# Gates of a mixer block in pairs by seven half-size products

## Chip, cores and metric

The kernel runs on 1 core of one Trainium2 chip. The metric is the time on the device in microseconds, the median of several executions.

## What is computed

One layer of a transformer-like block on 512 tokens of width 1024, in f32. The input is normalised (h) and multiplied by one wide matrix; the first columns feed four branches (attention, spatial gating, short convolution, pooling), the last 4096 columns are the pre-activations of four gates of width 1024. Then:

```python
gates = jax.nn.sigmoid(gate_pre + gate_b[l]).reshape(B_, S_, N_BRANCH, D_)
merged = (gates[:, :, 0] * y_a + gates[:, :, 1] * y_b
          + gates[:, :, 2] * y_c + gates[:, :, 3] * y_d)
x = x + rmsnorm(merged @ w_out[l], norm_mix_post[l])
h = rmsnorm(x, norm_ffn_pre[l])
f = jnp.square(jax.nn.relu(h @ w_ff1[l])) @ w_ff2[l]
x = x + rmsnorm(f, norm_ffn_post[l])
```

where y_a to y_d are the branches' outputs (256 wide) times a 256 x 1024 matrix each.

## The kernel before

Everything is kept transposed: features on the 128 partitions, the 512 tokens along the row. Each f32 operand is split into a high and a low piece of the type fp32r (`split_w`: ScalarE copies the high piece `wh`, VectorE subtracts for the low piece `wl`); `mm3` makes three TensorE products of every pair of operands, high by high, high by low, low by high. Weights come as tiles of 128 x 1024 f32 by SP's queue into a ring of three `raw` buffers and are split into five `wh`/`wl` buffers. `split_by_dma` (L122) spares VectorE the subtraction: ScalarE writes the negated high piece into `lo`, and a transfer that POOL issues adds the weight to it.

The scheduler of the framework orders each engine's instructions by priority (program order) as their inputs and buffers come free; TensorE alone keeps the order of the program (`InOrder`, L102), and ScalarE for a part of the head.

The stages, in order: the head, the branches and attention (to about 152 us); the gates; the output product with wO and the two norms; the feed-forward part; the end.

The gates (L679 to L682): for each of the 8 blocks b of 128 output features, four gate tiles (`gate`, L449; `feature_block`, L329: 8 K tiles x 3 products of 512 columns, tile `fb`, then a multiplication by the row `rbc` into a `g` tile), some of block 0 during attention. Then `merge(b)` (L457): four sigmoids, for each branch 6 products of 512 columns (tile `y`), multiplied by the gate and summed, the result split into `mh`, `ml`. L683 to L686 ask for gmix, gffn and x, which have room of their own, so that they come early.

The feed-forward part: the first `EARLY` = 4 tiles of w1 are multiplied by the first half of the tokens (`ff1`, L718, tile `z`) while the second half is still being normalised, then by the second half. The other 28 tiles go in pairs by a scheme of seven half-size products (Strassen's, in Winograd's form; L855 to L897): a pair is a 2 x 2 matrix of blocks (K halves by tile), the tokens' halves and K halves give the blocks A11, A12, A22 and the sums S1 to S4, made once. `part` (L849) is one step: 4 K tiles x 3 products of 256 columns into a bank `pa`, `pb`, `pc` or `pd`; VectorE makes four combinations of the weights in place in `raw`, and the results are put together from PSUM. Between the steps stand steps of the second product (`second`, L807, tile `acc`, 12 products of 512 columns).

Of the kernel before, what the change touches and what calls it, by code (L numbers as in the profile page):

```python
# [18 lines left out]
P = 128  # L19
S = 512  # L20
# [60 lines left out]
def build(ctx, tc, d, out):  # L81
# [40 lines left out]
    def split_by_dma(src):  # L122

        raw = load(src)
        hi = wp.tile([P, 1024], F32R, tag="wh", name="wh", bufs=5)
        lo = wp.tile([P, 1024], F32R, tag="wl", name="wl", bufs=5)
        ACT.copy(hi, raw)
        ACT.activation(lo, f(hi), AF.Copy, scale=-1.0)
        POOL.dma_start(lo, src.bitcast(F32R), accum_op=ALU.add)
        return hi, lo  # L130
# [187 lines left out]

    s3 = ExitStack()
# [349 lines left out]
    xp = ctx.enter_context(tc.tile_pool(name="xp", bufs=1, reuse_waits="tile", **right))  # L669
    x1 = xp.tile([P, NT, D], F32, name="x1")  # L670
    r2 = xp.tile([P, TOP], F32, name="r2")[:, :NT]
    mp = ctx.enter_context(ExitStack())
    mpool = mp.enter_context(tc.tile_pool(name="mp", bufs=1, reuse_waits="tile", **right))
    mh = mpool.tile([P, KD, S], F32R, name="mh")
    ml = mpool.tile([P, KD, S], F32R, name="ml")
    mT = (mh, ml)
    gmix = mpool.tile([P, D], F32, name="gmix")
    gffn = mpool.tile([P, D], F32, name="gffn")
# [17 lines left out]
    HK, HS = KD // 2, S // 2  # L696
# [9 lines left out]
    wk_ = ws.enter_context(tc.tile_pool(name="wk", bufs=1, reuse_waits="tile"))  # L706
# [316 lines left out]
```

## Time and profile before

| | us |
|---|---|
| median of 3 executions | 744.18 (743.61 to 745.3) |
| the profiled execution | 744.92 |
| its span in the profile | 743.2 |
| TensorE busy | 728.5 |
| VectorE busy | 467.2 |
| ScalarE busy | 356.5 |

The span is what the profile covers; the execution's own time is 1.7 us longer. Matmuls overlap in the engine, so the durations of single ones (389 ns for 512 columns) are longer than the time from one to the next. "Idle before" in a row is the time for which the engine did nothing before that instruction, and the name behind the arrow is what ended it. The windows view has the engines in the order TensorE (PE), its weight loads (PEld), VectorE (DVE), ScalarE (ACT), POOL, and behind them the granted TensorE clock as a share of full speed, the share of DMA time and GB/s.

### The profile page before, as it was taken

To read this page: it belongs to the slowest core of one execution; us is meant where nothing else is said; L and a number is where in the kernel's file an instruction comes from. 1 tells how busy PE (TensorE), PEld (TensorE's weight loads), DVE (VectorE), ACT (ScalarE), POOL (GpSimd) and SP (SyncE) were. 2 spreads that over 40 slices of the span, in tenths; PEclk is the share of its full clock that TensorE was granted. 3 is DMA by queue.
4 is the path that set the end of the run, shared out by engine and by line. 5 is a ranking of instruction groups with operands and counts; after the bars stand their busy time and mean duration, and the time that the engine had idled before them with its cause. 6 is when DMAs were issued, how large, how long until landed. Compare 5 with 4: busy or idle time off the path is not lost.

```text
span 743.2 us, 10315 instructions
## 1 busy us (share of the span) xinstructions
PE 728.5 (98%) x4058; PEld 636.4 (86%) x4058; DVE 467.2 (63%) x760; ACT 356.5 (48%) x584; POOL 15.9 (2%) x32
## 2 busy tenths in 40 slices
PE   8999999999999999999997999999999999999996
PEld 8998788888888888888887899999999999888885
DVE  7599986355456365365355976777677676774424
ACT  6875444523323232332346756546665556753411
POOL 1110000000000000000011000000000000000001
PEclk9999999999999999999999999999999999999999
DMA  8523222362232322323137033322433233533103
GB/s 304 183 107 114 86 95 73 117 219 94 90 109 86 112 86 90 109 86 111 44 101 198 1 108 120 101 99 86 130 97 114 86 101 127 170 113 112 60 0 114
DMA packets 23728, 80.87 MB, mean 109 GB/s; under 512 B 3072, under 2 KB 3584, under 8 KB 23680
## 3 DMA queue, kind: packets, MB, share of 16 engines
q1 hardware_dynamic: 23072, 78.12, 31.2%
q0 software_dynamic: 608, 2.10, 1.6%
q8 instruction: 32, 0.52, 0.3%
q14 instruction: 16, 0.13, 0.1%
HBM read 78.11 MB, written 2.10 MB: 108 GB/s over the span
## 4 chain that ended last, share of the span: by engine, by line
PE 88%; DVE 5%; DMA 2%; ACT 2%; issue 1%; SPq 0%; POOL 0%; DVEq 0%; ACTq 0%; POOLq 0%
PE fb L95 28%; PE acc L95 23%; PE pa L95 8%; PE y L95 6%; PE wo L95 5%; PE pc L95 5%; PE pd L95 3%; PE pb L95 2%; PE psA L95 2%; PE sgv L95 2%; DMA xT<-in_xT 1%; PE po L95 1%; DMA wl<-in_w 1%; DMA raw<-in_wF 1%; DVE wl L119 1%
## 5 line engine op out<-in xcount | busy, mean ns | idle before, releaser
L95 ACT CAST wh<-raw 128x1024 fp32r<-128x1024 f32 (+2 forms) x154 | 153.7, 1009 | 222.3 <-issue 105.4
L119 DVE TENSOR_TENSOR wl<-raw,wh 128x1024 fp32r<-128x1024 f32 (+2 forms) x150 | 173.8, 1167 | 28.8 <-ACT wh L95 26.5
L95 PE MATMUL fb<-zh,wh 128*128 128x512 f32 x336 | 131.4, 391 | 0.1
L95 PE MATMUL fb<-zl,wh 128*128 128x512 f32 x336 | 130.8, 389 | 0.0
L95 PE MATMUL fb<-zh,wl 128*128 128x512 f32 x336 | 130.8, 389 | 0.0
L95 PE MATMUL acc<-wh,ul 128*128 128x512 f32 x232 | 90.5, 390 | 1.2 <-DVE ul L798 1.2
L95 PE MATMUL acc<-wh,uh 128*128 128x512 f32 x232 | 90.7, 391 | 0.0
L95 PE MATMUL acc<-wl,uh 128*128 128x512 f32 x232 | 90.6, 391 | 0.0
L452 DVE TENSOR_TENSOR g<-fb,rbc 128x512 f32<-128x512 f32 x32 | 22.1, 692 | 96.7 <-PE fb L95 96.7
L798 DVE TENSOR_TENSOR ul<-u,uh 128x512 fp32r<-128x512 f32 x58 | 38.7, 689 | 57.2 <-ACT uh L95 57.1
L95 PEld LDWEIGHTS fb<-zh,wl 128*128 128x128 f32 x336 | 63.1, 188 | 13.2
L95 PEld LDWEIGHTS fb<-zh,wh 128*128 128x128 f32 x336 | 63.1, 188 | 13.2 <-DVE zc L361 0.4
L95 PEld LDWEIGHTS fb<-zl,wh 128*128 128x128 f32 x336 | 63.1, 188 | 12.8
L95 PEld LDWEIGHTS acc<-wh,ul 128*128 128x128 f32 x232 | 43.6, 188 | 11.4 <-DVE ul L798 2.1
L95 PEld LDWEIGHTS acc<-wh,uh 128*128 128x128 f32 x232 | 43.6, 188 | 8.5 <-ACT uh L95 0.4
L95 ACT CAST uh<-u 128x512 fp32r<-128x512 f32 x58 | 34.3, 618 | 34.2 <-PE acc L95 33.7
L95 PEld LDWEIGHTS acc<-wl,uh 128*128 128x128 f32 x232 | 43.6, 188 | 7.9
L95 ACT ACTIVATE u<-u 128x512 f32<-128x512 f32 x60 | 33.2, 622 | 16.3 <-DVE u L890 16.3
L95 PE MATMUL pa<-hsh,wh 128*128 128x256 f32 x112 | 31.3, 280 | 0.5 <-ACT x L95 0.5
L95 PE MATMUL pa<-hsl,wh 128*128 128x256 f32 x112 | 31.2, 279 | 0.0
L95 PE MATMUL pa<-hsh,wl 128*128 128x256 f32 x112 | 31.2, 279 | 0.0
L95 PE MATMUL wo<-wh,mh 128*128 128x512 f32 x64 | 25.1, 392 | 0.0
(313 smaller groups left out, 1419.7 us busy)
## 6 DMA issues: line engine op xcount, KB each, us to landing
raw<-in_w SPq DMA_DIRECT2D x64, 512.0 KB, 3.5
raw<-in_wG SPq DMA_DIRECT2D x32, 512.0 KB, 3.4
raw<-in_wF SPq DMA_DIRECT2D x10, 512.0 KB, 4.1
raw<-in_wB SPq DMA_DIRECT2D x8, 512.0 KB, 3.4
raw<-in_wO SPq DMA_DIRECT2D x8, 512.0 KB, 3.4
xk<-in_x SPq DMA_DIRECT2D x4, 512.0 KB, 9.3
x<-in_x SPq DMA_DIRECT2D x4, 512.0 KB, 5.8
wl<-in_w POOLq DMA_DIRECT2D x4, 512.0 KB, 6.5
```

The lines of the kernel that those rows point to most:

```text
L95: ins = op(*a, **k)
L119: DVE.tensor_tensor(lo[:, :n], raw[:, :n], f(hi)[:, :n], ALU.subtract)
L452: DVE.tensor_tensor(g, ps, rbc, ALU.mult)
L798: DVE.tensor_tensor(ul, u[j], f(uh), ALU.subtract)
```

## The change

Blocks 0 and 1 of the gates stay. For blocks 2 to 7 the seven-product scheme of the feed-forward part is made into a generator, `seven`, and the four gate tiles of a block go through it as two pairs. What that needs is added: `z_sums` makes the sums of z (`zsum`) during block 1, and the quarter of z that is used no more (first K half, second half of the tokens) is overwritten with the last form; the low piece of the right tile's second half (`w22`) is made by `split_by_dma`, also that of wB from block 1 on, in buffers of its own. `merge` becomes a generator as well: the products y of block b-1 are put between the steps of the first pair of block b. The merged result is kept in one tile for each block (`mT`) instead of one large tile, x, gmix and gffn get room that the gates used before, and are asked for when that is free. In the feed-forward part, `ff1` makes all products with the high piece of the weight first, tiles 2 and 3 of w1 are split by VectorE, the first tile of w2 is asked for before the first pair's weights, and the first three steps of the second product stand inside the first pair. The diff, cut:

```diff
--- before.py
+++ after.py
...
-    def split_by_dma(src):
-        raw = load(src)
-        hi = wp.tile([P, 1024], F32R, tag="wh", name="wh", bufs=5)
-        lo = wp.tile([P, 1024], F32R, tag="wl", name="wl", bufs=5)
-        ACT.copy(hi, raw)
-        ACT.activation(lo, f(hi), AF.Copy, scale=-1.0)
-        POOL.dma_start(lo, src.bitcast(F32R), accum_op=ALU.add)
+    def split_by_dma(src, raw=None, n=1024, own=None):
+        raw = load(src, n) if raw is None else raw
+        if own is None:
+            hi = wp.tile([P, 1024], F32R, tag="wh", name="wh", bufs=5)
+            lo = wp.tile([P, 1024], F32R, tag="wl", name="wl", bufs=5)
+        else:
+            hi, lo = [own.tile([P, 1024], F32R, tag=f"b{c}", name=f"b{c}", bufs=1) for c in "hl"]
+        ACT.copy(hi[:, :n], raw[:, :n])
+        ACT.activation(lo[:, :n], f(hi)[:, :n], AF.Copy, scale=-1.0)
+        POOL.dma_start(lo[:, :n], src.bitcast(F32R), accum_op=ALU.add)
...
+    HK, HS = KD // 2, S // 2
+    B1, B2 = slice(0, 512), slice(512, 1024)
+    def part(ps, w, at, a, first):
+        for k in range(HK):
+            mm3(ps[:, :HS], sl(w, slice(None), slice(at + k * P, at + (k + 1) * P)), sl(a, slice(None), k),
+                first and k == 0, k == HK - 1, not first)
+    def seven(srcs, forms, small, g, h, by_dma):
+        A11, A12, A22, S1, S2, S3, S4 = forms
+        left, rght = load(srcs[0]), load(srcs[1])
+        w = split_w(left)
+        w22 = split_by_dma(srcs[1][:, B2], rght[:, B2], 512) if by_dma else split_w(rght[:, B2], 512)
+        DVE.tensor_tensor(left[:, B1], rght[:, B1], left[:, B1], ALU.subtract)
+        DVE.tensor_tensor(rght[:, B1], rght[:, B2], rght[:, B1], ALU.subtract)
+        DVE.tensor_tensor(rght[:, B2], rght[:, B2], left[:, B1], ALU.subtract)
+        DVE.tensor_tensor(left[:, B2], left[:, B2], rght[:, B2], ALU.subtract)
+        wl = split_w(left)
+        wr = split_w(rght)
+        pa, pb = bank("pa"), bank("pb")
+        part(pa, w, 0, A11, True)
+        x1 = small()
+        ACT.copy(x1, pa[:, :HS])
+        yield
+        part(pb, w, 512, A12, True)
+        DVE.tensor_tensor(g[:, :HS], pb[:, :HS], x1, ALU.add)
+        yield
+        pc = bank("pc")
+        part(pc, wl, 0, S1, True)
+        x5 = small()
+        ACT.copy(x5, pc[:, :HS])
+        yield
+        part(pa, wr, 512, S2, False)
+        x2 = small()
+        ACT.copy(x2, pa[:, :HS])
+        yield
+        pd = bank("pd")
+        part(pd, wl, 512, A22, True)
+        yield
+        part(pc, w22, 0, S4, False)
+        DVE.tensor_tensor(h[:, :HS], pc[:, :HS], x2, ALU.add)
+        yield
+        part(pa, wr, 0, S3, False)
+        x3 = small()
+        ACT.copy(x3, pa[:, :HS])
+        DVE.tensor_tensor(g[:, HS:], pd[:, :HS], x3, ALU.add)
+        DVE.tensor_tensor(h[:, HS:], x3, x5, ALU.add)
+        yield
+    def forms(x, sums):
+        lo, hi, t0, t1 = slice(0, HK), slice(HK, KD), slice(0, HS), slice(HS, S)
+        return [sl(x, slice(None), k, t) for k, t in ((lo, t0), (hi, t0), (hi, t1))] + [
+            sl(sums, slice(None), c) for c in range(3)] + [sl(x, slice(None), lo, t1)]
...
-    def merge(b):
-        for i, g in enumerate(gates):
+    def merge(b, w):
+        gs = list(gates)
+        gates.clear()
+        for i, g in enumerate(gs):
             ACT.activation(g, g, AF.Sigmoid, bias=k1("gateb")[:, i * 8 + b:i * 8 + b + 1])
-        w = weights(d["wB"][b])
         prev = None
-        for i, br in ((1, bT), (2, cT), (3, dT), (0, aT)):
-            g = gates[i]
+        for i, br in ((1, bT), (2, cT), (3, dT), (0, aT)) if b == 0 else enumerate((aT, bT, cT, dT)):
+            g = gs[i]
             ps = bank("y")
             for k in range(2):
                 mm3(ps, sl(w, slice(None), slice((2 * i + k) * P, (2 * i + k + 1) * P)),
...
             if prev is not None:
                 DVE.tensor_tensor(g, g, prev, ALU.add)
             prev = g
-        ACT.copy(mh[:, b, :], prev)
-        DVE.tensor_tensor(ml[:, b, :], prev, f(mh)[:, b, :], ALU.subtract)
-        gates.clear()
+            yield
+        ACT.copy(mT[0][b], prev)
+        DVE.tensor_tensor(mT[1][b], prev, f(mT[0][b]), ALU.subtract)
...
+    zsum = [ss.tile([P, 3, HK, HS], F32R, name=f"zs{c}") for c in "hl"]
...
+    def z_sums(hh):
+        q = tqp.tile([P, 4, 2, HS], F32, name=f"q{hh}")
+        a11, a12, a21, a22 = (q[:, c] for c in range(4))
+        for c, (k, t) in enumerate(((0, 0), (HK, 0), (0, HS), (HK, HS))):
+            ix = slice(None), slice(k + 2 * hh, k + 2 * hh + 2), slice(t, t + HS)
+            DVE.tensor_tensor(q[:, c], f(zh)[ix], f(zl)[ix], ALU.add)
+        DVE.tensor_tensor(a22, a21, a22, ALU.add)
+        DVE.tensor_tensor(a21, a11, a21, ALU.subtract)
+        DVE.tensor_tensor(a11, a22, a11, ALU.subtract)
+        DVE.tensor_tensor(a12, a12, a11, ALU.subtract)
+        for c, v in enumerate((a22, a11, a21)):
+            ix = slice(None), c, slice(2 * hh, 2 * hh + 2)
+            ACT.copy(zsum[0][ix], v)
+            DVE.tensor_tensor(zsum[1][ix], v, f(zsum[0])[ix], ALU.subtract)
+        lower.append(a12)
+    steps = merge(0, weights(d["wB"][0]))
+    for i in range(4):
+        next(steps)
+    rest(steps)
+    for i in range(4):
+        gates.append(gate(1, i))
+        if i % 2 == 0:
+            z_sums(i // 2)
+    for hh, v in enumerate(lower):
+        ix = slice(None), slice(2 * hh, 2 * hh + 2), slice(HS, S)
+        ACT.copy(zh[ix], v)
+        DVE.tensor_tensor(zl[ix], v, f(zh)[ix], ALU.subtract)
+    tq.close()
+    merged("mp1", False)
+    ops = forms(z, zsum)
+    w = split_by_dma(d["wB"][1], own=wbp)
+    for b in range(2, KD):
+        steps = merge(b - 1, w)
+        for i in (0, 2):
+            g, h = (gp.tile([P, S], F32, tag="g", name="g", bufs=6) for _ in range(2))
+            for n, _ in enumerate(seven((d["wG"][4 * b + i], d["wG"][4 * b + i + 1]), ops, small_g, g, h, True)):
+                if i == 0 and n in (1, 2, 4, 5):
+                    next(steps)
+                if i == 0 and n == 5:
+                    rest(steps)
+                    w = split_by_dma(d["wB"][b], own=wbp)
+            for x in (g, h):
+                DVE.tensor_tensor(x, x, rbc, ALU.mult)
+            gates.extend((g, h))
+    rest(merge(KD - 1, w))
+    s4.close()
+    s1.close()
-    for b in range(KD):
-        while len(gates) < 4:
-            gates.append(gate(b, len(gates)))
-        merge(b)
-    nc.sync.dma_start(gmix, d["gmix"].partition_broadcast(P))
-    nc.sync.dma_start(gffn, d["gffn"].partition_broadcast(P))
-    for t in range(NT):
-        nc.sync.dma_start(x1[:, t, :], d["x"][t * P:(t + 1) * P, :])
-    s1.close()
...
+    gmix = wk_.tile([P, D], F32, name="gmix")
+    gffn = wk_.tile([P, D], F32, name="gffn")
+    nc.sync.dma_start(gmix, d["gmix"].partition_broadcast(P))
+    nc.sync.dma_start(gffn, d["gffn"].partition_broadcast(P))
+    for t in range(NT):
+        nc.sync.dma_start(x1[:, t, :], d["x"][t * P:(t + 1) * P, :])
...
     def ff1(j, w, ps, lo, hi):
-        for k in range(KD):
-            mm3(ps[:, lo:hi], sl(w, slice(None), slice(k * P, (k + 1) * P)), sl(h2, slice(None), k, slice(lo, hi)),
-                k == 0, k == KD - 1)
+        for c, parts in ((0, (0, 1)), (1, (0,))):
+            for k in range(KD):
+                for p in parts:
+                    PE.matmul(ps[:, lo:hi], w[c][:, k * P:(k + 1) * P], h2[p][:, k, lo:hi],
+                              start=c == 0 and k == 0 and p == 0, stop=c == 1 and k == KD - 1)
...
-        w, ps = split_by_dma(d["w1"][j]), bank("z")
+        w, ps = (split_by_dma if j < 2 else weights)(d["w1"][j]), bank("z")
...
-    w2 = {}
+    w2 = {0: weights(d["w2"][0, 0])}
     def second():
         j, us_ = pend.pop(0)
-        if j % 2 == 0:
+        if j and j % 2 == 0:
...
-        if j == EARLY - 1:
-            second()
...
+    ops = forms(h2, hsum)
     for j in range(EARLY, NFF, 2):
...
+        for n, _ in enumerate(seven((d["w1"][j], d["w1"][j + 1]), ops, small, g, h, False)):
+            if n == 4 or n in (1, 2) and j == EARLY:
+                second()
...
```

## Rows read from the trace of the kernel before

**Rows 1.** The page, part 1: busy time, share and instructions of each engine.
```profile
PE 728.5 (98%) x4058; PEld 636.4 (86%) x4058; DVE 467.2 (63%) x760; ACT 356.5 (48%) x584; POOL 15.9 (2%) x32
```

**Rows 2.** Windows: stretch, its length, each engine's busy time (instructions), clock, DMA.
```profile
157.32:179.08 21.76, 21.76 (x98) 18.02 (x97) 9.03 (x11) 6.67 (x9) 0.00 (x0) 1.00 0.43 154
184.52:347.72 163.20, 163.20 (x722) 135.13 (x721) 84.30 (x103) 50.34 (x61) 0.00 (x0) 1.00 0.29 97
392.90:406.50 13.60, 9.86 (x81) 9.45 (x80) 6.49 (x13) 8.08 (x14) 2.28 (x3) 1.00 0.94 219
406.50:425.80 19.30, 18.09 (x144) 17.24 (x143) 17.97 (x23) 13.77 (x23) 0.00 (x0) 1.00 0.03 13
460.05:475.35 15.30, 15.30 (x111) 14.31 (x110) 10.91 (x16) 9.04 (x16) 0.00 (x0) 1.00 0.33 101
```

**Rows 3.** The chain that ended last: start us, us, what, count.
```profile
157.32 21.76 PE fb L95 x96
179.08 5.44 PE y L95 x24
...
460.05 1.40 PE pa L95 x12
...
467.05 2.75 PE acc L95 x12
```

**Rows 4.** Timeline of VectorE, one feed-forward pair: start us, us, instruction, [idle before].
```profile
517.12 0.42 DVE L886 TENSOR_TENSOR u<-pc,x 128x256 f32<-128x256 f32 x1 [0.97 <-PE pc L95]
518.09 1.22 DVE L119 TENSOR_TENSOR wl<-raw,wh 128x1024 fp32r<-128x1024 f32 x1 [0.55 <-ACT wh L95]
519.49 1.22 DVE L119 TENSOR_TENSOR wl<-raw,wh 128x1024 fp32r<-128x1024 f32 x1 [0.18 <-ACT wh L95]
520.63 0.42 DVE L890 TENSOR_TENSOR u<-pd,x 128x256 f32<-128x256 f32 x1
520.97 0.41 DVE L891 TENSOR_TENSOR u<-x 128x256 f32<-128x256 f32 x1
523.83 1.29 DVE L798 TENSOR_TENSOR ul<-u,uh 128x512 fp32r<-128x512 f32 x2 [2.44 <-ACT uh L95]
...
525.57 2.36 DVE L119 TENSOR_TENSOR wl<-raw,wh 128x1024 fp32r<-128x1024 f32 x2
527.97 0.69 DVE L861 TENSOR_TENSOR raw<-raw 128x512 f32<-128x512 f32 x1
528.69 0.69 DVE L862 TENSOR_TENSOR raw<-raw 128x512 f32<-128x512 f32 x1
```

**Rows 5.** Timeline of VectorE, the merge of block 7.
```profile
344.37 1.36 DVE L468 TENSOR_TENSOR g<-g,y 128x512 f32<-128x512 f32 x2
...
349.12 1.22 DVE L119 TENSOR_TENSOR wl<-raw,wh 128x1024 fp32r<-128x1024 f32 x1
350.26 0.68 DVE L473 TENSOR_TENSOR ml<-g,mh 128x512 fp32r<-128x512 f32 x1
```

**Rows 6.** Timeline of ScalarE, a feed-forward pair.
```profile
475.20 2.20 ACT L95 ACTIVATE u<-u 128x512 f32<-128x512 f32 x4 [1.36 <-DVE u L890]
...
486.42 1.06 ACT L95 CAST wh<-raw 128x1024 fp32r<-128x1024 f32 x1 [3.52 <-PE pc L95]
```

**Rows 7.** The page, part 6: a gate weight's load, count, size, us to landing.
```profile
raw<-in_wG SPq DMA_DIRECT2D x32, 512.0 KB, 3.4
```

**Rows 8.** The tile `wl`: its four POOL transfers, from issue to landing.
```profile
DMA to landing us min/median/max: 5.6/6.5/7.6
```

**Rows 9.** Timeline of TensorE, the first products of the feed-forward part.
```profile
399.48 0.39 PE L95 MATMUL z<-hh,wl 128*128 128x256 f32 x1 [2.48 <-DMA wl<-in_w]
...
403.83 0.39 PE L95 MATMUL z<-hh,wl 128*128 128x256 f32 x1 [1.26 <-DMA wl<-in_w]
...
406.39 0.28 PE L95 MATMUL z<-hh,wl 128*128 128x256 f32 x1
```

**Rows 10.** Timeline of VectorE at the same place.
```profile
407.77 1.29 DVE L731 TENSOR_TENSOR hl<-tr,hh 128x512 fp32r<-128x512 f32 x2 [5.20 <-ACT hh L95]
```

More of the change, by code (lines that the diff above doesn't have):

```diff
@@ L668, in build @@
     TOP = 20
-    xp = ctx.enter_context(tc.tile_pool(name="xp", bufs=1, reuse_waits="tile", **right))
-    x1 = xp.tile([P, NT, D], F32, name="x1")
[L671 to L677, printed above, removed]
@@ L678, in build, with merged @@
-    gffn = mpool.tile([P, D], F32, name="gffn")
-    for b in range(KD):
-        while len(gates) < 4:
-            gates.append(gate(b, len(gates)))
-        merge(b)
-    nc.sync.dma_start(gmix, d["gmix"].partition_broadcast(P))
-    nc.sync.dma_start(gffn, d["gffn"].partition_broadcast(P))
-    for t in range(NT):
-        nc.sync.dma_start(x1[:, t, :], d["x"][t * P:(t + 1) * P, :])
-    s1.close()
-    HK, HS = KD // 2, S // 2
+    mp = ctx.enter_context(ExitStack())
+    mT = [], []
+    def merged(name, pad):
+        pool = mp.enter_context(tc.tile_pool(name=name, bufs=1, reuse_waits="tile", **right))
+        for b in range(HK):
+            for c in range(2):
+                mT[c].append(pool.tile([P, S], F32R, name=f"m{'hl'[c]}{len(mT[c])}"))
+        if pad:
+            pool.tile([P, TOP], F32, name="top")
@@ new lines, in build, with small_g, rest @@
+    merged("mp0", True)
+    s4 = ExitStack()
+    wbp = s4.enter_context(tc.tile_pool(name="wbp", bufs=1, reuse_waits="tile"))
+    ss = s4.enter_context(tc.tile_pool(name="ss", bufs=1, reuse_waits="tile"))
+    ss.tile([P, 8], F32, name="shift")
+    zsum = [ss.tile([P, 3, HK, HS], F32R, name=f"zs{c}") for c in "hl"]
+    def small_g():
+        return ss.tile([P, HS], F32, tag="x", name="x", bufs=5)
+    def rest(steps):
+        for _ in steps:
+            pass
+    while len(gates) < 4:
+        gates.append(gate(0, len(gates)))
@@ new lines, in build @@
+    tq = ExitStack()
+    tqp = tq.enter_context(tc.tile_pool(name="tq", bufs=1, reuse_waits="tile", **right))
+    lower = []
+    def z_sums(hh):
[13 more added lines that the diff above has]
+        lower.append(a12)
@@ L697, in build @@
+    rest(merge(KD - 1, w))
+    s4.close()
+    s1.close()
+    xp = ctx.enter_context(tc.tile_pool(name="xp", bufs=1, reuse_waits="tile"))
+    x1 = xp.tile([P, NT, D], F32, name="x1")
+    r2 = xp.tile([P, lines(NT)], F32, name="r2")[:, :NT]
     hs = ExitStack()
@@ L745, in build @@
             for k in range(KD):
-                mm3(ps, sl(mT, slice(None), k, slice(t * P, (t + 1) * P)),
+                mm3(ps, sl([m[k] for m in mT], slice(None), slice(t * P, (t + 1) * P)),
                     sl(wo[k // 2], slice(None), slice((k % 2) * 512, (k % 2 + 1) * 512)), k == 0, k == KD - 1)
@@ L847, in small @@
         return fx.tile([P, HS], F32, tag="x", name="x", bufs=5)
-    def part(ps, w, at, a, first):
-        for k in range(HK):
-            mm3(ps[:, :HS], sl(w, slice(None), slice(at + k * P, at + (k + 1) * P)), sl(a, slice(None), k),
-                first and k == 0, k == HK - 1, not first)
+    ops = forms(h2, hsum)
     for j in range(EARLY, NFF, 2):
         g, h = u[j], u[j + 1]
-        left, rght = load(d["w1"][j]), load(d["w1"][j + 1])
-        w = split_w(left)
-        w22 = split_w(rght[:, B2], 512)
-        DVE.tensor_tensor(left[:, B1], rght[:, B1], left[:, B1], ALU.subtract)
-        DVE.tensor_tensor(rght[:, B1], rght[:, B2], rght[:, B1], ALU.subtract)
-        DVE.tensor_tensor(rght[:, B2], rght[:, B2], left[:, B1], ALU.subtract)
-        DVE.tensor_tensor(left[:, B2], left[:, B2], rght[:, B2], ALU.subtract)
-        wl = split_w(left)
-        wr = split_w(rght)
-        pa, pb = bank("pa"), bank("pb")
-        part(pa, w, 0, A11, True)
-        x1_ = small()
-        ACT.copy(x1_, pa[:, :HS])
-        part(pb, w, 512, A12, True)
-        DVE.tensor_tensor(g[:, :HS], pb[:, :HS], x1_, ALU.add)
-        if j == EARLY:
-            second()
-        pc = bank("pc")
-        part(pc, wl, 0, S1, True)
-        x5 = small()
-        ACT.copy(x5, pc[:, :HS])
-        part(pa, wr, 512, S2, False)
-        x2 = small()
-        ACT.copy(x2, pa[:, :HS])
-        pd = bank("pd")
-        part(pd, wl, 512, A22, True)
-        second()
-        part(pc, w22, 0, S4, False)
-        DVE.tensor_tensor(h[:, :HS], pc[:, :HS], x2, ALU.add)
-        part(pa, wr, 0, S3, False)
-        x3 = small()
-        ACT.copy(x3, pa[:, :HS])
-        DVE.tensor_tensor(g[:, HS:], pd[:, :HS], x3, ALU.add)
-        DVE.tensor_tensor(h[:, HS:], x3, x5, ALU.add)
```

7 lines of the change are left out of this document (1 added, 6 removed).

## The prediction

> **What bounds the kernel now.** I read the totals first: TensorE is busy for 728.5 of 743.2 us [rows 1], so only less TensorE time, or one of its few gaps, can shorten the run. The stretches of the windows view come next [rows 2]. In blocks 2 to 7 (184.52 to 347.72) TensorE is busy for all of 163.20 us at a granted clock of 1.00 (the 2.4 GHz level), while VectorE works 84.30 and ScalarE 50.34 us. A busy TensorE can hide overlapping records, so the chain of waits gives the true pace [rows 3]: four gate tiles, 96 products of 512 columns, take 21.76 us, which is 226.7 ns a product; a step of 12 products of 256 columns takes 1.40 us, 116.7 ns each. The y products of a block take 5.44 us. A block is therefore 27.20 us of pure TensorE pace, and six blocks are 163.2 us. The one other place where TensorE visibly waits is the start of the first feed-forward product, 9.86 busy of 13.60 us [rows 2].
>
> **The products.** A pair of gate tiles is 48 products of 512 columns, half of 21.76: 10.88 us. The scheme has seven steps of 12 products of 256 columns: 7 x 1.40 = 9.80 us. That is 1.08 us less for a pair, and there are 12 pairs: **-12.96 us**. The pace of the half-size step is not assumed: the feed-forward pairs run the same `part` steps, with the same three passes, at 1.40 us without a gap [rows 3]. A block becomes 2 x 9.80 + 5.44 = 25.04 us; its y steps now lie inside the first pair of the next block and still cost 1.36 each.
>
> **VectorE in these blocks.** This is where the gain can be lost. The feed-forward pair is the model of a pair's work [rows 4]; I count from start to start, since the ends overlap. Three low pieces of 1024: two take 2.36, so 3.54. Four combinations, each fed by the one before: 0.72 each, 2.88. Four sums of 256 columns out of PSUM: 0.34 each, 1.36. Two multiplications by `rbc`: 0.68 each (two PSUM operations in 1.36 [rows 5]), 1.36. Together 9.14 us. A merge takes 4.75 us from the first multiplication (344.37) to what follows its last sum (349.12), and 0.68 for the low piece: 5.43 [rows 5]; its weight's low piece moves to a transfer. A block asks VectorE for 2 x 9.14 + 5.43 = 23.71 of 25.04 us, 95%. Before, it had 84.30 of 163.20, 52%. ScalarE is no bound: the feed-forward pair has 9.04 us of it [rows 2], of which 2.20 are activations that a gate pair has not [rows 6], so under 7 us a pair; with four sigmoids, a merge copy and wB a block needs some 19 of 25.
>
> Does 95% stop TensorE? In the feed-forward pair VectorE waits four times: 0.97 for a product, 0.55 and 0.18 for ScalarE's copies, 2.44 for the u split [rows 4]. The last has no counterpart here. The first is VectorE being early. The other two follow copies that begin when a product frees a buffer of `wh` [rows 6], again because everything is ahead of TensorE. Such waits shrink when VectorE falls behind, so they do not add to 95%. Following one block by hand with five `wh` buffers and no w2 tile among them: the low piece of the next pair's `wl` can be written about 2.3 us after the fifth product and is needed 5.6 us after it at the soonest; `wr` the same one product later. About 3 us of slack for each pair. The `raw` ring of three is the other loop: the next right half loads when `wl` is split (3.4 us [rows 7]), then half a copy, four combinations, a copy [rows 6] and a split: 3.4 + 0.5 + 2.9 + 1.06 + 1.2 = 9.1 us, inside even the short pair of 9.80. I take 0.25 us lost a block, **+1.5 us**; the bounds are 0 and, if the 1.70 us of waits that have a counterpart all stayed, 23.71 + 3.40 = 27.1 a block, 6 x 2.07 = 12.4.
>
> **The transfers that POOL issues.** The low piece of `w22` and of wB needs a copy, a negation and an accumulating transfer. The four in the trace landed 5.6 to 7.6 us after issue [rows 8]. `w22` is used in the sixth product; from the time its buffer frees (the second product of the pair before) that is 9 us more than the 9 or 10 it needs. I cost it at nothing; were it late by x, each pair would pay x, and nothing excludes a small price.
> A rule of the Trainium skill speaks against it: "SBUF — State Buffer", section on the two separate sides, says that a transfer issued by GpSimd can wait for its descriptors while VectorE runs certain operations, those in a two-port mode. By that rule a VectorE at 95% would delay `w22`; the page excepts the tensor_tensor that these blocks consist of, and in this trace three of the four transfers were issued in a stretch where VectorE was busy for 6.49 of 13.60 us and the slowest landed in 7.6 us, which shows no such delay. Transfers landing in 20 us would put the pairs back to no gain.
>
> **From block 1 to block 2.** The sums of z are new: 22 VectorE operations of 512 elements at 0.68 = 15.0 us, and two low pieces for the last form. The third product of the first pair needs them at 179.08 + 2.80 + 1.36 = 183.2. From 157.32 VectorE has 26 us; it must still do the last sum and the low piece of merge 0 (1.4), four gate multiplications (2.8), the sums (15.0) and for the first pair one split, four combinations and one split (5.2): 24.4 us. It does fit, barely; the split weights of block 1 are ready before, as the five `wh` buffers run ahead. Bounds: 0, and 5 us if half of the sums come after the gates. A gain is excluded, as TensorE has no gap there [rows 2]. I take **+1.0 us**.
>
> **The end of the gates.** gmix, gffn and the four x tiles are now asked for after the last gates, on SP, ahead of the wO tiles in program order. The x tiles are used half of the output product later. gmix takes the place of gate tiles, so it starts about when the last merge ends and lands 3.4 to 7.6 us later by the transfers of that size [rows 7, 8], about when the first output tile of 5.44 us is read; eight PSUM banks cover the rest. If the wO loads stood behind it on SP, the price would be a load, a copy and a split, 3.4 + 1.06 + 1.18 = 5.6 us. They have buffers while the last pair runs, so I take 0.
>
> **The start of the feed-forward part.** TensorE waits 2.48 and 1.26 us for low pieces that a POOL transfer brings [rows 9]. The new `ff1` runs 16 products of a tile before it needs the low piece, and tiles 2 and 3 are split by VectorE. With the piece landing at 399.48 as before, tile 1 has 8 products left (0.94), tile 2 takes 2.80: it ends at 403.2 where it ended at 406.5 [rows 9]: -3.3. Against it: VectorE gets two splits more (2.36), in front of a stretch where it is busy for 17.97 of 19.30 us [rows 2]; it was idle for 5.20 us up to 407.77 [rows 10], so they fit ahead. The 2.75 us of second-product steps that stood ahead of the first pair now stand in it, so its weights are due sooner; w2's tile, asked for early, no longer competes with them. Bounds: -4.5 (the 1.2 us that TensorE lacks from 406.5 to 425.8 [rows 2] gone too) and +1.8 (both splits and the missing cover on the path). I take **-3.0 us**. The matmuls after that are the same.
>
> Sum: -12.96 + 1.5 + 1.0 - 3.0 = -13.5 us. The profiled execution took 744.92 us, 0.74 over the median of 744.18; so 731.4 for such an execution and **730.7** as a median.
>
> **The rivals.** *VectorE sets the pace in part.* For it: 95%, and copies on two engines feeding each other. Against it: the same helper runs without a gap in the feed-forward pairs at 71% (10.91 of 15.30). At 26 to 27.1 us a block the loss is 5.8 to 12.4 instead of 1.5: 735 to 741.6.
> *VectorE's waits take over, and it is slower.* The place is VectorE's order in the short pair, which has no y steps as cover: sums that wait for the sixth and seventh products stand ahead of splits that TensorE needs. From 1.75 us of waiting a pair the products' gain is gone (27.2 us a block), from about 1.9 the whole run is longer than before. With 2.5 us it would be 23.71 + 5.0 = 28.7 a block, 6 x 1.5 = 9 us over, less the 2.0 of the other terms: 751. The feed-forward pair's whole idle time of 4.39 shows that such waits exist; that 2.44 of it belong to u speaks against.
> *The transfers of `w22` come late.* Each pair waits at its sixth product; 1 us late is 12 us in all, 742.7. Against it: 9 us of slack.
>
> **How the numbers follow.** Forecast, 726.5 to 735: 0.66. VectorE in part, 735 to 742.7: 0.20. Within 0.2% (1.5 us, what measurement can tell from no change), from any mixture: 0.03. Slower by VectorE's waits: 0.09. Transfers late, half of it on each side: 0.02. The low end is the forecast with all bounds at their best (-12.96 - 4.5 from 744.18, 726.7); the high end takes in the first rival whole, 741.6. Faster 0.87, same 0.03, slower 0.10.
>
> **What would show it.** Right: steps of 1.40 us for pa, pb, pc, pd between about 179 and 328; a block of 25 to 25.4 us; VectorE near 95% there; the waits of z gone but for about 1.1 us. Wrong: TensorE waiting for `wl` in these blocks, most of all in the second pair of a block; a gap at the first pair of block 2 behind the sums of z; a gap at the first wo product; waits for a transfer at pc's second use. If half-size steps between y steps take clearly more than 1.40, the first term is wrong.

## The result and the profile after

The changed kernel takes **735.08 us** (median of four runs, 733.82 to 736.25), the kernel before 743.96 in the same runs: a ratio of 0.9877, with a 95% interval of 0.9852 to 0.9902. That is 8.9 us less. The forecast was 730.7, 13.3 us less than the median before; the time lies inside the range, 4.4 us above the forecast. It also lies 0.08 us over 735, where the forecast's own stretch of times ends and that of the first rival (VectorE sets the pace in part) begins; whether that rival's mechanism came is asked below. Of the four executions the two longer ones, 736.25 and 736.09, had a mean granted clock of 0.992 to 0.993 and the two shorter ones 0.997, and the profiled one is the longest. The profiled execution took 736.25 us with a span of 734.5, where before's span was 743.2: the two traces differ by 8.7 us, and this is what has to be found in them.

Part 1 of the page of the kernel after, which answers [rows 1]:

```profile
PE 719.9 (98%) x4490; PEld 648.3 (88%) x4490; DVE 532.5 (72%) x887; ACT 404.8 (55%) x681; POOL 30.4 (4%) x49
```

TensorE is still busy 98% of the span; VectorE went from 63 to 72%. The windows of the kernel after, with the columns of [rows 2]: block 1's gates, two whole blocks of gates, the first feed-forward products, the start of the first feed-forward pair:

```profile
157.00:178.76 21.76, 21.76 (x97) 18.02 (x96) 11.81 (x16) 8.06 (x11) 0.88 (x1) 1.00 0.35 83
205.73:231.23 25.50, 25.50 (x195) 24.47 (x194) 22.12 (x35) 16.04 (x25) 2.56 (x3) 1.00 0.57 144
256.73:282.23 25.50, 25.50 (x195) 24.47 (x194) 22.37 (x36) 16.00 (x25) 2.57 (x3) 1.00 0.56 145
385.04:393.61 8.57, 8.57 (x75) 8.57 (x74) 7.52 (x15) 5.39 (x11) 0.56 (x1) 1.00 0.83 240
408.49:425.00 16.51, 13.27 (x64) 11.23 (x63) 11.12 (x16) 7.39 (x12) 0.00 (x0) 0.79 0.26 95
```

In the blocks TensorE never waits, although VectorE works for 22.1 to 22.4 of 25.50 us, 87%. A block takes 25.50 where 25.04 was worked out. The first 72 feed-forward products, 12.83 us before with the waits of [rows 9], take 8.57 with none. And the last row has a loss that was not there: 16.51 us in which TensorE is busy for 13.27 at a granted clock of 0.79.

Read by the places where TensorE begins each stretch (us, before and after):

| stretch | before | after | difference |
|---|---|---|---|
| block 1's gate tiles are done | 178.92 | 178.79 | -0.1 |
| from there to the first wo product | 168.6 | 158.5 | -10.1 |
| first 144 products of wo | 32.64 | 34.25 | +1.6 |
| first 72 products of z | 12.83 | 8.57 | -4.3 |
| from there to the third feed-forward pair | 53.37 | 57.59 | +4.2 |

The starts come from TensorE's timeline; the chain of [rows 3] has the same places 0.16 us later. First before, then after: the first product behind block 1's gate tiles, the first of wo, the first of z, and the third pair:

```profile
178.92 0.39 PE L95 MATMUL y<-bh,wh 128*128 128x512 f32 x1
...
347.56 0.39 PE L95 MATMUL wo<-wh,mh 128*128 128x512 f32 x1
...
393.69 0.37 PE L95 MATMUL z<-hh,wh 128*128 128x256 f32 x1
...
459.89 0.28 PE L95 MATMUL pa<-hh,wh 128*128 128x256 f32 x1
```
```profile
178.79 0.28 PE L95 MATMUL pa<-zh,wh 128*128 128x256 f32 x1
...
337.31 0.39 PE L95 MATMUL wo<-wh,mh 128*128 128x512 f32 x1
...
385.04 0.37 PE L95 MATMUL z<-hh,wh 128*128 128x256 f32 x1
...
451.20 0.28 PE L95 MATMUL pa<-hh,wh 128*128 128x256 f32 x1
```

The sum is -8.7, the whole difference of the spans. So the gates gave 10.1, the output product took 1.6 back, and the start of the feed-forward part gave 4.3 and took the same again within one pair.

**Where the gates fall short.** TensorE's timeline of the kernel after, one step `pb` in block 4 (start us, us, instruction):

```profile
231.23 0.28 PE L95 MATMUL pb<-zh,wh 128*128 128x256 f32 x1
...
232.55 0.28 PE L95 MATMUL pb<-zh,wl 128*128 128x256 f32 x1
232.67 0.40 PE L95 MATMUL y<-ah,bh 128*128 128x512 f32 x1
```

The 12 products take 232.67 - 231.23 = 1.44 us, not the 1.40 of the feed-forward pairs [rows 3]. The steps that read `z` itself (pa's first product, pb, pd, pc's second) take 1.43 to 1.44, those that read the sums `zs` 1.41 on the mean, a y step between them 1.385 for 1.36. A block has eight of the first, six of the second and four of the third: 8 x 1.437 + 6 x 1.41 + 4 x 1.385 = 25.50.

**The wait in the output product.** TensorE's wait in the timeline, and VectorE's and ScalarE's timelines at the same place; the bracket is the idle time before and what ended it:

```profile
343.27 0.50 PE L95 MATMUL wo<-wh,mh 128*128 128x512 f32 x1 [1.04 <-ACT mh L95]
```
```profile
333.89 2.48 DVE L119 TENSOR_TENSOR wl<-raw,wh 128x1024 fp32r<-128x1024 f32 x2 [2.15 <-ACT wh L95]
...
341.16 1.41 DVE L540 TENSOR_TENSOR g<-g 128x512 f32<-128x512 f32 x2
```
```profile
332.81 1.05 ACT L95 CAST wh<-raw 128x1024 fp32r<-128x1024 f32 x1 [2.66 <-DMA raw<-in_wO]
```

The last merge's result `mh` is 1.04 us late for the eighth K tile of the first wo product. Ahead of the sums that make it, VectorE splits two wO tiles, and these waited for ScalarE's copy, which waited 2.66 us for the load of wO. The late thing is the load. The chain that ended last shows what it waited for, two splits on VectorE that free a `raw` buffer:

```profile
327.40 2.28 DVE wl L119 x2
...
329.69 4.29 DMA raw<-in_wO
```

**The first feed-forward pair.** The chain that ended last, kernel after (start us, us, what), TensorE's two waits in its timeline, and the windows of the same place:

```profile
414.85 0.70 DVE raw L347
...
415.57 1.05 ACT wh L95
...
416.65 1.24 DVE wl L119
...
417.93 2.50 PE pc L95 x10
420.44 4.54 PE acc L95 x12
424.98 1.40 PE pa L95 x12
```
```profile
416.67 0.38 PE L95 MATMUL pc<-hsh,wh 128*128 128x256 f32 x1 [2.48 <-ACT wh L95]
...
417.93 0.58 PE L95 MATMUL pc<-hsh,wl 128*128 128x256 f32 x1 [0.76 <-DVE wl L119]
```
```profile
408.49:416.00 7.51, 5.71 (x38) 4.87 (x36) 7.47 (x13) 4.50 (x9) 0.00 (x0) 1.00 0.00 0
416.00:418.00 2.00, 0.56 (x3) 0.37 (x3) 1.49 (x3) 2.00 (x3) 0.00 (x0) 0.83 0.00 0
418.00:422.00 4.00, 4.00 (x15) 3.61 (x16) 2.15 (x2) 0.89 (x2) 0.00 (x0) 0.50 0.64 231
422.00:425.00 3.00, 3.00 (x11) 2.38 (x10) 0.00 (x0) 0.00 (x0) 0.00 (x0) 0.64 0.58 216
```

VectorE is busy for 7.47 of 7.51 us up to 416; the four combinations of the first pair's weights come last in that queue, and TensorE waits 2.48 us for the copy and 0.76 for the split behind them. After these waits the granted clock falls to 0.50, the 1.2 GHz level, and 12 products of w2 take 4.54 us instead of 2.75 [rows 3]. The pair takes 27.42 us (408.49 to 435.91) where its products need 7 x 1.40 + 4 x 2.75 = 20.8: 6.6 lost, 3.24 in the waits and the remaining 3.4 by the clock, as the windows' shares give it too: 2 x 0.17 + 4 x 0.50 + 3 x 0.36 = 3.4. Before, the same products lost 2.4 (1.6 with the step ahead of this pair, 0.8 in the next). The difference is the +4.2 of the table.

What the clock takes differs. In five of the runs below, with the changed gates and the same start of the feed-forward part, TensorE has the same two waits, 2.46 to 2.48 and 0.76 us, but the half clock lasted about half as long, and the pair took 26.0 to 26.1 us. The stretch at half clock in one of them, the run with one wB:

```profile
416.00:419.40 3.40, 3.15 (x12) 2.96 (x13) 2.47 (x3) 1.21 (x2) 0.00 (x0) 0.50 0.57 170
```

**The transfers that POOL issues** were in time. The last column is us from issue to landing, part 6 of the page of the kernel after:

```profile
bl<-in_wB POOLq DMA_DIRECT2D x7, 512.0 KB, 7.7
wl<-in_wG POOLq DMA_DIRECT2D x12, 256.0 KB, 4.3
```

By the rule of the Trainium skill ("SBUF — State Buffer", section on the two separate sides) that the prediction weighed, a busy VectorE could hold these back. With VectorE at 87%, all of it tensor_tensor, the 256 KB of `w22` landed in 4.3 us. The transfers of [rows 8] are twice that size; those of the same 512 KB, for wB, took 7.7 us at the median where [rows 8] has 6.5, so like for like they are 1.2 us slower, far from the 20 us that would have taken the gain. No step of TensorE waits for one. The trace agrees so far with the page's exception for that operation.

### The profile page after: what moved, and what is told of

It reads as the page before. It is cut to its first block, busy times and chain, and to the rows that moved or that the text cites. A ratio compares the mean times of both kernels' runs of the same rounds, so it can differ in the third digit from the quotient of the medians.

```text
span 734.5 us, 11480 instructions
## 1 busy us (share of the span) xinstructions
PE 719.9 (98%) x4490; PEld 648.3 (88%) x4490; DVE 532.5 (72%) x887; ACT 404.8 (55%) x681; POOL 30.4 (4%) x49
## 4 chain that ended last, share of the span: by engine, by line
PE 71%; DVE 19%; ACT 4%; DMA 3%; issue 2%; SPq 0%; POOL 0%; DVEq 0%; ACTq 0%
PE acc L95 24%; PE pa L95 10%; PE fb L95 9%; PE pc L95 7%; PE wo L95 5%; DVE wl L119 5%; PE pd L95 3%; PE pb L95 3%; PE y L95 2%; ACT wh L95 2%; PE psA L95 2%; PE sgv L95 2%; PE z L95 1%; DMA raw<-in_wG 1%; DVE g L540 1%
## 5 line engine op out<-in xcount | busy, mean ns | idle before, releaser
L95 ACT CAST wh<-raw 128x1024 fp32r<-128x1024 f32 (+2 forms) x171 | 165.3, 980 | 145.8 <-PE pc L95 52.6
L119 DVE TENSOR_TENSOR wl<-raw,wh 128x1024 fp32r<-128x1024 f32 (+2 forms) x157 | 181.7, 1169 | 41.8 <-ACT wh L95 39.2
L95 PE MATMUL fb<-zh,wh 128*128 128x512 f32 x144 | 56.7, 394 | 0.1
L95 PE MATMUL fb<-zh,wl 128*128 128x512 f32 x144 | 56.2, 390 | 0.1
L95 PE MATMUL fb<-zl,wh 128*128 128x512 f32 x144 | 56.1, 390 | 0.0
L95 ACT COPY x<-pa 128x256 f32<-128x256 f32 x78 | 28.4, 366 | 8.8 <-PE pa L95 7.2
L95 PEld LDWEIGHTS fb<-zh,wl 128*128 128x128 f32 x144 | 27.0, 188 | 6.2 <-DVE wl L119 0.5
L95 PEld LDWEIGHTS fb<-zh,wh 128*128 128x128 f32 x144 | 27.1, 188 | 5.7 <-DVE zc L429 0.4
L95 PEld LDWEIGHTS fb<-zl,wh 128*128 128x128 f32 x144 | 27.1, 188 | 5.3
L95 ACT ACTIVATE g<-g,c 128x512 f32<-128x512 f32 x32 | 22.5, 721 | 10.4 <-DVE g L815 10.3
```

Of the source, the lines that this page charges most:

```text
L95: ins = op(*a, **k)
L119: DVE.tensor_tensor(lo[:, :n], raw[:, :n], f(hi)[:, :n], ALU.subtract)
```

## The experiments

The four runs of the kernel after spread over 2.4 us, so a single run's total tells little of an edit worth one or two; what follows rests on steps and waits in the traces.

**Does the place of z in SBUF set the pace?** In the built program `wh` and `wl` begin at multiples of 64 bytes, and so does `z`; the sums `zs` and the feed-forward `hh` lie 32 bytes off, behind a tile `shift` of 32 bytes. Two runs move one of them each, the weights staying where they are. In the first, the tiles allocated behind `z`, the operands of the y products among them, move by the same 32 bytes.

```
+    zp.tile([P, 8], F32, name="shift")
     zh = zp.tile([P, KD, S], F32R, name="zh")
...
-    ss.tile([P, 8], F32, name="shift")
     zsum = [ss.tile([P, 3, HK, HS], F32R, name=f"zs{c}") for c in "hl"]
```

> After the change a step of 12 products takes 1.43 to 1.44 us where the moving operand is z (p1, p2, p5, p6; 283 ns a product in the groups) and 1.40 to 1.42 where it is the sums of z (p3, p4, p7; 280 ns). Theory: the place of z in SBUF sets this. z starts at a multiple of 64 bytes, as the weights do; the sums of z and the feed-forward operand start 32 bytes beside one. Here z is moved by 32 bytes and the sums keep their residue. Theory expects all steps at 1.40 to 1.41, a block of 25.2 instead of 25.50 us, gates 1.5 to 2 us shorter, total about 733. Rival (TensorE is slowed by what VectorE and the transfers do beside it in this stage): steps of z stay at 1.44, total as after, 735.

Measured: 735.34 us (before 744.72). The same step in that run's timeline, and its chain of waits from the gates of block 1 on:

```profile
231.62 0.28 PE L95 MATMUL pb<-zh,wh 128*128 128x256 f32 x1
...
232.90 0.28 PE L95 MATMUL pb<-zh,wl 128*128 128x256 f32 x1
```
```profile
157.63 22.40 PE fb L95 x96
180.03 1.40 PE pa L95 x12
```

The twelfth product starts 1.28 us after the first, where it was 1.32 (232.55). The steps now take 1.40, a block 25.2: the pace goes with where z lies. But the 512-column products of blocks 0 and 1 go the other way, 96 of them 22.40 instead of the 21.76 of [rows 3], so block 2 begins 1.1 us later (its first product at 179.87, after has 178.79). And in the last blocks steps of 1.55 and 1.81 appear (pc at 298.74 and 324.16). The wait stands at the step behind each, TensorE's and ScalarE's timelines at the second one:

```profile
325.97 0.39 PE L95 MATMUL pa<-zsh,wh 128*128 128x256 f32 x1 [0.25 <-ACT x L95]
```
```profile
324.07 1.05 ACT L95 CAST wh<-raw 128x1024 fp32r<-128x1024 f32 x1 [1.55 <-DMA raw<-in_wO]
```

TensorE waits for ScalarE's copy out of `pa`, which stands on ScalarE behind a copy that waited 1.55 us for its load. From pb of block 2 to the wo product it is 155.86 us where after has 157.08, 1.2 us less; in the total, expected at 733, it can't be seen.

The second run only takes away the `shift` ahead of `zs`:

> The opposite of moving z: the sums of z are put on a multiple of 64 bytes too, z stays. Theory (place in SBUF): the steps with the sums (p3, p4, p7) rise from 1.40-1.42 to 1.44, a block from 25.50 to about 25.7, total up by 0.5 to 1.4 us. Rival (other work in the stage): nothing changes.

Measured: 735.31 us. The steps that read the sums take 1.44 like the others, a block is 25.68 (205.64 to 231.32). Together the two runs show that a 256-column step takes 1.40 with its moving operand 32 bytes off and 1.44 with it at the multiple of 64, the weights staying where they are. The total did not move by a measurable amount.

**The first feed-forward pair.** The prediction named the second-product steps that stood ahead of this pair as its cover. This run puts two of them behind the pair's second product, and none behind its third:

```
-            if n == 4 or n in (1, 2) and j == EARLY:
+            for _ in range(2 if n == 1 and j == EARLY else n == 4):
                 second()
```

> In the first feed-forward pair two steps of the second product stand between p2 and p3 instead of one there and one after p3; nothing else is moved. After the change TensorE waited 2.5 and 0.8 us before p3 for the weight wl, which VectorE reaches only at 417.9, and ran at half the granted clock until 424.8. Theory: the missing cover of 2.75 us is what this costs, directly and through the clock; expected: p3 waits about 1 us or less, no stretch at half clock, total 4 to 6 us lower (729 to 731). Rival (VectorE's chain is late whatever stands before p3, and the following steps wait as well): the wait moves to p4 or later, gain under 2.75.

Measured: 732.9 us. TensorE's one wait left there, and the windows around it:

```profile
420.17 0.39 PE L95 MATMUL pc<-hsh,wl 128*128 128x256 f32 x1 [0.76 <-DVE wl L119]
```
```profile
412.00:416.00 4.00, 4.00 (x26) 3.58 (x25) 4.00 (x7) 2.84 (x7) 0.00 (x0) 1.00 0.00 0
416.00:420.00 4.00, 3.41 (x16) 2.55 (x14) 3.45 (x6) 2.82 (x4) 0.00 (x0) 1.00 0.00 0
```

The clock stays at 1.00 here, and from the first z product to the third pair it is 60.62 us instead of 66.16: 5.5 us less by an exchange of order alone, with VectorE as full as before (4.00 of 4.00 us). What was missing was 2.75 us of TensorE's work in front of pc. The span is 3.3 us less than that of the kernel after (731.2 for 734.5): z began 2.2 us later here, as the output product took 36.69 us. Its wait for `mh` was 1.9 us in this run, and the clock fell behind that one:

```profile
345.00:352.00 7.00, 7.00 (x25) 5.61 (x24) 0.85 (x2) 0.69 (x2) 0.00 (x0) 0.76 0.40 160
```

**The feed-forward start taken apart.** One run undoes the new start and keeps the gates; the other adds the new start to the kernel before. The edit of the first, with `ff1` put back too (the second is its reverse, on the kernel before):

```
-        w, ps = (split_by_dma if j < 2 else weights)(d["w1"][j]), bank("z")
+        w, ps = split_by_dma(d["w1"][j]), bank("z")
...
-    w2 = {0: weights(d["w2"][0, 0])}
+    w2 = {}
...
+        if j == EARLY - 1:
+            second()
...
-            if n == 4 or n in (1, 2) and j == EARLY:
+            if n == 4 or n == 1 and j == EARLY:
```

> The change's gates alone: the start of the feed-forward part is as before (four tiles split by a transfer, the old order of products in ff1, w2 asked for late, one step of the second product before the first pair). Theory: the parts add up, and the feed-forward start gave nothing net in the change (4.3 us won at tile z, 4.2 lost at the first pair through the missing cover and the half clock), so this kernel takes about what the whole change takes, 734 to 736; the z products wait again (about 12.8 us for 72), and the first pair loses under 3 us. Rival (the feed-forward start was worth its 3 us and the gates lost more than I read): 738 to 739.

Measured: 737.03 us (before 744.5), 1 us above the stretch expected. The z products again wait 2.6 us for the transfer and take 12.94; from z to the third pair it is 66.74 us.

> The kernel before with the new start of the feed-forward part alone: tiles 2 and 3 split by VectorE, high pieces first in ff1, w2's first tile asked for early, the steps of the second product in the order of the change. Theory: as in the change, z gains about 4 us and the first pair loses about as much, with a wait before p3 and a stretch at half clock: 743 to 745, no difference from before (744.7 in the same set). Rival (the loss at the first pair comes from the new gates, through VectorE's or SP's backlog): here the gain shows, 740 to 741.

Measured: 743.63 us. The end of its chain in the first pair:

```profile
426.66 1.45 PE pc L95 x10
428.10 4.33 PE acc L95 x12
```

With the old gates the new start has the same 2.5 and 0.8 us of waits and the same slow w2 step, 4.33. From z to the third pair it is 64.88 where before has 66.20. So the new start by itself brings 1.3 us beside the old gates. Beside the new ones it brings 0.6 us in the profiled execution (66.74 to 66.16) and 1.6 to 2.0 in the five runs with the shorter stretch at half clock (64.8 to 65.2). And the loss in the first pair is its own doing, not that of the new gates.

**The wait of the output product.** The first two wo tiles do their K tiles 0 to 6 first, and K tile 7, the last merge's, afterwards:

```
+                for i in range(2):
+                    first[i] = bank("wo")
+                    wo_k(first[i], i, range(KD - 1))
...
+                wo_k(ps, t, range(KD - 1, KD))
```

> The first two tiles of the output product make their K tiles 0 to 6 first and K tile 7, which needs the last merged block, afterwards: 4.8 us of cover for the last merge. After the change the output product waited 1.0 us there and took 34.25 us for its first 144 products, before 32.64. Theory (the last sums stand on VectorE behind a split of wO that waits for its load, so the last merge is late): the wait goes, 1.0 to 1.6 us gained there, total about 733.5. Rival (the loss is not the wait but the transfers of x, gmix and gffn beside these products): the 144 products still take over 33.5 us.

Measured: 734.96 us. The chain's row:

```profile
337.65 32.64 PE wo L95 x144
```

The 144 products take what they took before, so the transfers of x, gmix and gffn beside them cost nothing. With the wait go its 1.04 us of idle time and the 0.6 us by which the products at it followed each other more slowly. The total was expected at 733.5; the first feed-forward pair has its waits and a long stretch at half clock here too, and takes 27.0 us.

**Is VectorE near its limit?** Here `w22`'s low piece is made by VectorE, not by a transfer (the last argument of `seven` is False in the gates), 0.68 us more for each pair:

> The gates' w22 is split by VectorE and not by ScalarE and a transfer: 0.68 us more VectorE work a pair, 1.36 a block, and no transfer in the pairs. After the change a block takes 25.50 us and TensorE waits for nothing in it. Theory (VectorE at 95% is within a few per cent of being the bound; my count gives 23.71 + 1.36 = 25.07): the blocks stay near 25.5 or begin to show waits for wl, 0 to 4 us in all, total 735 to 739. Rival (VectorE has much more room than my count says): nothing changes. Second rival (the transfers slow the stage): faster than after.

Measured: 735.63 us. A block of it in the windows view:

```profile
256.73:282.23 25.50, 25.50 (x194) 24.47 (x193) 23.30 (x37) 14.39 (x24) 0.85 (x1) 1.00 0.42 124
```

At 23.3 of 25.50 us, 91%, the blocks still take 25.50. VectorE's load does not set the blocks' pace, and neither `w22`'s transfers nor their absence is felt in them.

**What makes wO late?** In the kernel after, the loads that open each block start at 204.73, 230.60, 256.76, 282.29 and 308.40, on the mean every 25.9 us; TensorE needs 25.50. The 25.9 is no fixed amount: with z moved the loads came every 25.6 us for a block of 25.17, again some 0.4 behind. The suspect is the ring of three `raw` buffers, through which the four gate tiles and wB of a block pass with load, copy, combinations and split. This run takes one of the five tiles out:

```
                 if i == 0 and n == 5:
                     rest(steps)
-                    w = split_by_dma(d["wB"][b], own=wbp)
```

> Blocks 2 to 7 all use the weight tile wB of block 1: the six reloads of wB, with their copy, negation and accumulating transfer, are left out, so the ring of three `raw` buffers turns four times a block instead of five (part of the computation is left out). Theory (the ring of raw buffers with its loads, copies, combinations and splits is the slow loop: 25.9 us a block against TensorE's 25.50, so the last gate weights and wO come late): the first load of a block comes every 25.5 us or less, set by TensorE's products freeing wh; the wO splits and the last sums are done earlier, and TensorE's wait of 1.0 us for mh in the output product shrinks to under 0.3, the first 144 products taking 32.7 to 33.2 instead of 34.25. Rival (mh is late because the chain behind the last product, four sums and copies and a split, is longer than the products that cover it, whatever the weights do): the wait stays at 1.0 us, 34.2. Blocks 25.50 by both, since no load sets TensorE's step.

Measured: 732.97 us (before 745.51). The first request for wO on SP in the kernel after and in this run, and TensorE's longest waits in this run (us in total, times, longest):

```profile
320.62 16.11 SPq L112 DMA_DIRECT2D raw<-in_wO  x8
```
```profile
307.87 26.69 SPq L112 DMA_DIRECT2D raw<-in_wO  x8
```
```profile
PE pc L95 <- ACT wh L95: 2.5, 1, 2.5
...
PE pc L95 <- DVE wl L119: 0.8, 1, 0.8
```

wO is asked for 12.75 us earlier, while TensorE reaches the wo product at 337.24 instead of 337.31. The wait for `mh` is gone, and the 144 products take 32.65. The six traces with this order of products and all of wB had waits of 0.41 to 1.90 us there. So it is the preparation of the weights that was late, not the chain behind the last product. The edit also takes wB's copy and negation off ScalarE, 2.1 us a block, and its transfers; whether the turn of the buffers alone would have done it was not told apart. The same with z moved:

> The same, and z moved by 32 bytes as in the run that moved z alone (six reloads of wB left out). Theory (with z moved TensorE's block of 25.18 is shorter than the ring's turn, which is why waits appeared in the last blocks): with the shorter ring all six blocks keep 25.1 to 25.2 and the products from pb of block 2 to the output product take about 155.0 instead of 155.86; no step of pc or pa above 1.45. Rival (the late waits come from VectorE's sums, not from the ring): the steps of 1.5 to 1.8 us at the last blocks stay, 155.8.

Measured: 732.53 us. Every half-size step takes 1.39 to 1.41, the late ones of the run with z alone moved are gone, and from pb of block 2 (181.53) to the wo product (336.64) it is 155.11 us.

The place of z is then worth 2.0 us in the gates (158.47 to 156.51 from pa on), of which block 2's later start (180.13 for 178.77) takes 1.4.

**A better version.** The two orders that helped, two steps of w2 ahead of pc and K tile 7 last, and a transfer for `w22` in the first feed-forward pair, which takes half a split, 0.68 us, out of VectorE's queue there:

```
-        for n, _ in enumerate(seven((d["w1"][j], d["w1"][j + 1]), ops, small, g, h, False)):
-            if n == 4 or n in (1, 2) and j == EARLY:
+        for n, _ in enumerate(seven((d["w1"][j], d["w1"][j + 1]), ops, small, g, h, j == EARLY)):
+            for _ in range(2 if n == 1 and j == EARLY else n == 4):
                 second()
```

> The change with its two losses mended: K tile 7 of the first two output tiles last; two steps of the second product between p2 and p3 of the first feed-forward pair; w22 of that pair by a transfer, which takes 0.68 us off VectorE ahead of wl. Theory: the wo loss (1.6) and the first pair's loss (5.5 to 6) are separate and add up: 727 to 729, faster than the change by 6 to 8 us. Rival (the gain of one moves the wait on, as VectorE's chain is the bound of both): 731 to 733.

Measured: **728.45 us** (five runs, 727.7 to 729.06), before 744.5: ratio 0.9781, interval 0.9768 to 0.9794. TensorE's waits over the whole run (us in total, times, longest):

```profile
PE psA L95 <- ACT wah L95: 1.6, 2, 0.8
PE warm L95 <- DVE warm L164: 1.1, 1, 1.1
PE psA L95 <- DVE wah L290: 0.8, 1, 0.8
PE pa L95 <- ACT x L95: 0.8, 1, 0.8
```

The first three are at the kernel's start, where after has the same ones. The 144 products of wo take 32.64. The waits for `mh` and in front of pc are gone; what is left in the feed-forward part is 0.8 us in the second pair. Against the profiled run of the kernel after (736.25 to 729.06, 7.2 us less): the output product 1.6, from z to the third pair 5.2 (66.16 to 60.96), and 0.4 from the wo product's earlier start (336.92). The transfer for `w22` gave nothing: with the two w2 steps alone this stretch took 60.62 us, and the 0.8 us that went from in front of pc came back in the second pair. The two changes of order carry the gain.

## Why the prediction was right, and where it was short

The sign and the bulk were right: the products of the gates carry the gain, and TensorE sets the pace in the blocks. The median, 735.08, falls on the edge of the times given to the rival of VectorE in part, but its mechanism did not come: a block took 25.50 us, not 26 to 27.1, and TensorE waited for nothing in it. Step by step, in the profiled executions' us:

- **The products, -12.96: -10.1 to -10.2.** The count of steps and the model were right, the pace was mis-sized. It was taken from pairs whose operands lie elsewhere; a block is 25.50, not 25.04, and 6 x 0.46 = 2.8 us of the gain are not there. The prediction named clearly slower steps as what would make this term wrong. Moving z showed the cause of 2.0 us of this. The other 0.8 are mostly the y steps, 1.385 us between half-size steps where the two last ones in a row take 1.36; why was not tested.
- **VectorE, +1.5: 0.** No wait appears at 87% nor, with `w22` put on it, at 91%. The bill of 23.71 us a block was above the measured 21.8 to 22.4. The rivals built on VectorE had the wrong place: what fell behind was the loop of load, copy, combinations and split through the ring of `raw`, which the prediction timed at 9.1 us for one turn of a pair's right half inside 9.80. It left out that wB takes a fifth turn in each block. VectorE near 95% was one of its signs of being right, and it was 87%.
- **`w22`'s transfers, 0: 0.** They land in 4.3 us. One reading of the trace before was off: in the stretch named, two of the four transfers were issued and not three; POOL's other instruction there is a tensor_tensor, and the third issue stands at 391.84, 1 us ahead.
- **From block 1 to block 2, +1.0: -0.1.** The sums fitted; TensorE has no gap.
- **The end of the gates, 0: +1.6.** The step looked at gmix and the SP queue, and those were harmless. It took the wO loads to have free buffers in time; that loop had fallen behind by then, and the late wO held up VectorE's queue in front of the last sums. Shown by one wB less (wait gone) and by K tile 7 done last (wait avoided). A gap at the first wo product was among the signs of being wrong, and it came.
- **The start of the feed-forward part, -3.0: 0** (-1.0 to -1.5 in the five runs with the shorter stretch at half clock). The first half was right and small: z gave 4.3 us where 3.3 was worked out. The second was named and then left out of the value: the missing 2.75 of second-product steps. It stood only in the bound of +1.8. Counted from the first z product TensorE came to the pair 8.5 us sooner (23.45 us instead of 31.95), 4.3 by z and 4.2 by the step taken out of its way and the wait in it, and VectorE, full until 416, was not ready; 3.24 us of waits followed, and in the profiled execution the clock's fall doubled them. No bound had a price for the clock. The run with two w2 steps in front shows that the order alone decides it.

Off by +2.8 - 1.5 - 1.1 + 1.6 + 3.0 = 4.8, by which the profiled execution (736.25) lies over 731.4. That the miss is not larger is in part luck: the two allowances that were not needed, 1.5 for VectorE and 1.0 for the way into block 2, hid a third of the 7.4 us that the other steps missed.

What stays open: why a product's pace depends on where its moving operand lies. For the half-size and gate products the runs moved that operand and not the weights, so whether its place by itself or against the weights counts was not told apart. Open as well: why the clock's fall lasts twice as long in some executions as in others with the same waits.

## What to carry to other kernels

When TensorE's work in front of a point is made shorter or moved behind it, ask what else reaches that point at a time of its own: here VectorE's queue did not get shorter, and most of what the faster start won came back as waits and as a lower clock. A loop that prepares weights must be timed over a whole block with every tile that passes through its buffers, since a loop 0.4 us a block behind shows nothing until its lead is used up. And a pace read from one place of a kernel holds for another only with the same shapes and the same places in SBUF.

## What the runs showed of the hardware

- A 256-column product took 120.0 ns (1.44 / 12) with the moving operand at a multiple of 64 bytes and 116.7 ns (1.40 / 12) with it 32 bytes off. For 512 columns it was the reverse: 226.7 ns (21.76 / 96) and 233.3 ns (22.40 / 96). The Trainium skill ("TensorE: Matmul & The Clock Gate", section "Back-to-back issue gap") gives N / 2.4 + 2.5 for the gap of a single product, by which I estimate 109 and 216 ns, and 131 ns as the sustained figure at 512 columns. All four rows of this case lie above these, and the rows decide.
- Two waits of 2.48 and 0.76 us, 0.5 us apart, were followed by half the granted clock in all eight traces that have them (0.47 for 0.76 in one). In the profiled execution of the kernel after that cost 3.4 us, as much again as the waits; in six others, with a shorter stretch at half clock, 2.0 to 2.1.
- Single waits went either way. After 1.9 us (the run with two w2 steps in front, output product) the clock fell, to 0.76 on the mean from 345 to 352, and after 2.6 us (the run with the old feed-forward start, first z products) to 0.57 from 391 to 395. After 0.76 us alone in the first of these runs, after 1.04 to 1.48 us for `mh` in four other runs, and in the kernel before after the 2.48 and 1.26 us of [rows 9] it stayed at 1.00.
